# Causal mask of MLA scores: from a matrix product on TensorE into VectorE's row-maximum pass

## The chip, the core and the metric

The kernel runs on one core of one Trainium2 chip. A core has a matrix engine (TensorE, PE in the profile, with its weight loads as PEld), a vector engine (VectorE, DVE), a scalar engine (ScalarE, ACT), a general engine (GpSimd, POOL), and DMA queues that SyncE (SP), ScalarE and GpSimd issue. Each engine works through its own queue in order; semaphores order the engines among each other. The metric is the time of one execution on the device in microseconds (us), as the median of several runs.

## The reference, cut to what matters

The reference computes one layer of a hybrid decoder on 512 tokens of width 1024: a layer norm, a token mixer of gated linear attention (GLA, 4 heads) and multi-head latent attention (MLA, 8 heads) side by side, merged by gates and projected, then a squared-ReLU MLP of hidden width 4096, each with a residual and a layer norm. What the change touches is the causal softmax of MLA:

```python
for blk in range(seq // Q_BLOCK):                  # 4 blocks of 128 queries
    q0, q1 = blk * Q_BLOCK, (blk + 1) * Q_BLOCK
    s = (jnp.einsum('bhqd,bhkd->bhqk', q_nope[:, :, q0:q1], k_nope[:, :, :q1])
         + jnp.einsum('bhqr,bkr->bhqk', q_rope[:, :, q0:q1], k_rope[:, :q1]))
    s = s.astype(jnp.float32) * scale
    mask = (q0 + jnp.arange(Q_BLOCK))[:, None] >= jnp.arange(q1)[None, :]
    p = jax.nn.softmax(jnp.where(mask, s, -jnp.inf), axis=-1).astype(v.dtype)
    outs.append(jnp.einsum('bhqk,bhkv->bhqv', p, v[:, :, :q1]))
```

Block i reads keys 0 to 128(i+1). Only the last 128 of these keys need a mask, the triangle of the diagonal block.

## The kernel before, in words

All large products are made from operands split into a high and a low part: `hi` is the value rounded to TensorE's fp32r format by ScalarE, `lo` the rest by VectorE, and a product is the sum of hi x hi, hi x lo and lo x hi. Products with features on the partitions go through `gemm_fm` (lines 231 to 233), products with tokens on the partitions through `gemm_tm` (lines 264 to 266). Weights are streamed: SyncE's queue loads a block (`wraw`, line 168, three buffers), ScalarE makes `whi` (line 180) and VectorE `wlo` (line 181), two buffers each, while TensorE works on the block before. A block cannot be split before TensorE has freed a buffer.

The stages follow each other: input norm and latents, the GLA projections with the GLA heads between them, the gates, the output projection of GLA (`y_gla`), the MLA heads in four pairs, the output projection of MLA (`y_mla`), the merge, and the MLP. The heads are Python generators: `tick` advances them between the products of the stage's projections, so that TensorE always has projection products to fill in with. That gives each instruction its place in program order; a planner then writes the queue of each engine by priority and by its own estimate of the times, and gives out the buffers. All instructions are unrolled, and the order in which an engine works is fixed before the run.

An MLA head is `mla_head`. For each of the 4 query blocks it makes a score tile of 128 queries by n = 128, 256, 384 or 512 keys in a PSUM bank (pool `px`, four banks that the transposes share): five products at lines 830 to 834, of the two parts without and the two parts with rotation. The sixth product, line 835, adds the mask to the diagonal block: the identity in bf16 (`identb`) times `negb`, a bf16 table of 0 and -1e30. VectorE takes the negated row maximum `mx` from the bank (line 837). ScalarE takes exp(score + mx) from the bank into an SBUF tile `Pm` (line 840) and sums the rows on the way (`sme`). VectorE inverts the sum (line 841) and scales the tile (line 842). TensorE transposes the tiles (line 854), they are split, and the products with the values follow (lines 873 to 875). `Pm` comes from the pool B of 22 buffers of 128 x 512 fp32; blocks 0 and 2 share one.

`identb` is made by ScalarE at the start (line 393) from the constants, `negb` by VectorE in `prep` (line 418) from `neg`, a 128 x 128 fp32 table that comes by DMA in `cb`.

`lmask` (line 400) holds the level masks of GLA as bytes, 7 levels x 2 x 2 x 64 = 1792 bytes per partition. VectorE fills it in two casts at line 912 and reads it in the GLA heads (lines 652 and 685). The GLA heads are finished by `finish(*t_gla)`, line 974, before `y_gla(0)`; the MLA heads begin behind that.

Of the kernel before, what the change touches and what calls it, by code (L numbers as in the profile page):

```python
# [10 lines left out]
F32 = mybir.dt.float32  # L11
F32R = mybir.dt.float32r
BF = mybir.dt.bfloat16
I32 = mybir.dt.int32
U8 = mybir.dt.uint8
AF = mybir.ActivationFunctionType
ALU = mybir.AluOpType
AX = mybir.AxisListType

P = 128  # L20
T = 512
# [25 lines left out]
LEVELS = (1, 2, 4, 8, 16, 32, 64)  # L47
# [5 lines left out]
def tile_hybrid_block(ctx: ExitStack, tc: tile.TileContext, I, out, dbg=None):  # L53
    nc = tc.nc
    dbg = dbg or {}
    consts = ctx.enter_context(tc.tile_pool(name="consts", bufs=1))
# [8 lines left out]
    def nm(s):  # L65
        uid[0] += 1
        return f"{s}_{uid[0]}"
# [4 lines left out]
    def A(shape, dt=F32, n="a"):  # L72
        tag, bufs = ("C", 8) if n in TAG_C else (n, TAG_W[n]) if n in TAG_W else ("A", 24)
        return pa.tile(shape, dt, tag=tag, bufs=bufs, name=nm(n))

    def B(shape, dt=F32, n="b"):
        return pb.tile(shape, dt, tag="B", name=nm(n))

    def S(shape, dt=F32, n="s"):
        return sm.tile(shape, dt, tag=n, name=nm(n))  # L80
# [4 lines left out]
    def PX(shape=(P, T), dt=F32, n="px"):  # L85
        return px.tile(list(shape), dt, tag="px", name=nm(n))
# [4 lines left out]
    act = nc.scalar.activation  # L91
# [4 lines left out]
    mm = nc.tensor.matmul  # L96
# [7 lines left out]
    def split(src, hi, lo, scale=None):  # L104
        if scale is None:
            act(hi, src, AF.Copy)
            return vtt(lo, src, f(hi), op=ALU.subtract)
        else:
            act(hi, src, AF.Copy, scale=scale)
            return stt(lo, src, scale, f(hi), op0=ALU.mult, op1=ALU.subtract)  # L110
# [13 lines left out]
    ident = ca[:, 0:P]  # L124
# [2 lines left out]
    mhalf = consts.tile([P, 8], F32, name="mhalf")  # L127
    nc.vector.memset(mhalf, -0.5)
    identr = consts.tile([P, P], F32R, name="identr")
    identb = consts.tile([P, P], BF, name="identb")  # L130
    negb = consts.tile([P, P], BF, name="negb")


    stream = []
# [65 lines left out]
    def step(g):  # L200
        try:
            next(g)
        except StopIteration:
            active.remove(g)
# [7 lines left out]
    def finish(*gs):  # L212
        while any(g in active for g in gs):
            for g in list(active):
                if g in gs:
                    step(g)
# [173 lines left out]


    act(identr, ident, AF.Copy)
    act(identb, ident, AF.Copy)
    cb = consts.tile([P, PACK_B], F32, name="cb")
    nc.scalar.dma_start(cb, I["c_pack_b"])
    cut = np.cumsum([0, 3, 2, NK, GH, 2 * NK, NK, NK, P, 32]).tolist()
    qag, kvg, glg, bga, bgt, ln1g, ln1b, neg, invf = [cb[:, cut[i]:cut[i + 1]] for i in range(9)]
    posi = consts.tile([P, NT], I32, name="posi")
    nc.scalar.dma_start(posi, I["positions"].rearrange("(t p) -> p t", p=P))
    lmask = consts.tile([P, len(LEVELS), 2, 2, 64], U8, name="lmask")  # L400
    lmi = A([P, 2, len(LEVELS), 64], I32, "lmi")
    nc.scalar.dma_start(lmi[:, 0], I["c_lmask"])
    wa2 = B([80, T], F32, "wa2")
# [7 lines left out]
    def prep():  # L411
        with tc.issue_after(st["pow"].ins):
            nc.gpsimd.memset(lmi[:, 1], 0)
        for li, s in enumerate(LEVELS):
            nc.gpsimd.dma_start(lmi[s:, 1, li], I["c_lmask"][:P - s, li])
        with tc.issue_after(last_in.ins):
            vts(hbg, bgt, 0.5, None, op0=ALU.mult)
            nc.vector.tensor_copy(negb, neg)
        posf = consts.tile([P, NT], F32, name="posf")
        with tc.issue_after(last_in.ins):  # L420
            nc.vector.tensor_copy(posf, posi)
        ang = B([P, NT, 32], F32, "ang")
        for tt in range(NT):
            vts(ang[:, tt, :], invf, posf[:, tt:tt + 1], None, op0=ALU.mult)
        yield
        angs = []
        for sh in (0.0, 0.25):
            kq = B([P, NT, 32], F32, "kq")
            vts(kq, ang, 1.0 / (2.0 * math.pi), sh, op0=ALU.mult, op1=ALU.add)
            vts(kq, kq, MAGIC, None, op0=ALU.add)  # L430
            vts(kq, kq, MAGIC, None, op0=ALU.subtract)
            r = B([P, NT, 32], F32, "rr")
            stt(r, kq, -TWO_PI_1, ang, op0=ALU.mult, op1=ALU.add)
            stt(r, kq, -TWO_PI_2, r, op0=ALU.mult, op1=ALU.add)
            stt(r, kq, -TWO_PI_3, r, op0=ALU.mult, op1=ALU.add)
            vts(r, r, sh * 2.0 * math.pi, PI_F, op0=ALU.add, op1=ALU.min)
            vts(r, r, -PI_F, None, op0=ALU.max)
            angs.append(r)
            yield
        act(sn2[:, :, 32:], angs[0], AF.Sin)  # L440
        act(cs2[:, :, :32], angs[1], AF.Sin)
        nc.vector.tensor_copy(cs2[:, :, 32:], cs2[:, :, :32])
        vts(sn2[:, :, :32], sn2[:, :, 32:], -1.0, None, op0=ALU.mult)
        yield
# [325 lines left out]
    scale = HQ ** -0.5  # L770
# [47 lines left out]
    def mla_head(h, hl, qn, kn, vt):  # L818
        for _ in range((0 if h == MH - 1 else STAG) * hl):
            yield  # L820
        KK, qs = KKs[0], QS[h]
        Ps = []
        P02 = B([P, T], F32, "P02")
        for i in range(NT):
            n = P * (i + 1)
            nn = max(n, 2 * P)
            c = slice(i * P, (i + 1) * P)
            p = PX()
            o = p[:, :nn]
            mm(o, qn[:, 0, c], kn[:, 0, :nn], start=True, stop=False)  # L830
            mm(o, qn[:, 0, c], kn[:, 1, :nn], start=False, stop=False)
            mm(o, qn[:, 1, c], kn[:, 0, :nn], start=False, stop=False)
            mm(o, qs[:, c], KK[:, 0, :nn], start=False, stop=False)
            mm(o, qs[:, c], KK[:, 1, :nn], start=False, stop=False)
            mm(p[:, c], identb, negb, start=False, stop=True)
            mx = S([P, 1], F32, "mx")
            nc.vector.tensor_reduce(mx, p[:, :n], axis=AX.X, op=ALU.max, negate=True)
            Pm = P02[:, :P] if i == 0 else P02[:, P:] if i == 2 else B([P, T], F32, "Pm")
            sme = S([P, 1], F32, "sme")
            act(Pm[:, :n], p[:, :n], AF.Exp, bias=mx, accum_out=sme)  # L840
            nc.vector.reciprocal(sme, sme)
            vts(Pm[:, :n], Pm[:, :n], sme, None, op0=ALU.mult)
            Ps.append(Pm)
            if i != 0:
                yield

        PT = [A([P, 2, T], F32R, "PT0"), A([P, 2, T], F32R, "PT1"), B([P, 2, 256], F32R, "PT2")]
        plan_t = ([(i, 0, i) for i in range(4)], [(i - 1, 1, i) for i in range(1, 4)] + [(3, 3, 3)],
                  [(i - 2, 2, i) for i in range(2, 4)])
        for b, (pl, pt) in enumerate(zip(plan_t, PT)):  # L850
            n = len(pl) * P
            p = PX()
            for cc, j, i in pl:
                nc.tensor.transpose(p[:, cc * P:(cc + 1) * P], Ps[i][:, j * P:(j + 1) * P], ident)  # L854
            split(p[:, :n], pt[:, 0, :], pt[:, 1, :])
            if b != 1:
                yield
        PT0, PT1, PT2 = PT
        while vt[NT - 1] is None:
            yield  # L860
        o = PX()
        for j in range(NT):
            c = slice(hl * P, (hl + 1) * P)
            vh, vl = vt[j][:, 0, c], vt[j][:, 1, c]
            if j == 0:
                ph, pl, od = PT0[:, 0, :], PT0[:, 1, :], o
            elif j == 1:
                ph, pl, od = PT1[:, 0, :384], PT1[:, 1, :384], o[:, 128:]
            elif j == 2:
                ph, pl, od = PT2[:, 0, :], PT2[:, 1, :], o[:, 256:]  # L870
            else:
                ph, pl, od = PT1[:, 0, 384:], PT1[:, 1, 384:], o[:, 384:]
            mm(od, vh, ph, start=j == 0, stop=False)
            mm(od, vh, pl, start=False, stop=False)
            mm(od, vl, ph, start=False, stop=j == NT - 1)
        yield
        om = A([P, 2, T], F32R, "omT")
        st["om"] = split(o, om[:, 0, :], om[:, 1, :])
        omT[h] = om
# [17 lines left out]
    for hf in range(2):  # L897
        if hf == 1:
            finish(t_ln1)
            t_prep = spawn(prep())  # L900
        for i in range(2):
            gemm_tm([PL["lat", i]], hT, half, ev_lat(i), tts=(2 * hf, 2 * hf + 1))
# [46 lines left out]
    def y_gla(mb):  # L949
        def ev_y(a, ps):  # L950
            g = gt[mb * 4 + a]
            stt(g[:, 0, :], g[:, 0, :], 1.0, ps, op0=ALU.add, op1=ALU.mult)
        gemm_fm(PL["yg", mb], ogT, T, ev_y)
# [18 lines left out]
    omT_lazy = Lazy()  # L972

    finish(*t_gla)
    WID[0] = 2
    y_gla(0)
    WID[0] = 4
# [330 lines left out]
```

## Time and profile before

| | before |
|---|---|
| median of 3 runs | 894.29 us (894.25 to 894.30) |
| the profiled execution | 893.91 us |
| its span, first to last instruction | 891.8 us |
| mean clock granted to TensorE | 0.997 |
| TensorE busy | 869.8 us, 98% of the span |
| VectorE busy | 579.0 us, 65% |
| ScalarE busy | 432.2 us, 48% |
| GpSimd busy | 170.7 us, 19% |
| mask products, line 835 | 32, from 357.6 to 461.2 us |

A row of the profile that groups instructions names the line, the engine and the operation, then out<-in by the names of the program's tiles, the shapes, the count, and behind the bar the busy time in us, the mean duration of one in ns, and the idle time of the engine just before them with what ended it. A row of one line's instructions (`L835 PE MATMUL ... x32: 218/230/232`) gives minimum, median and maximum in ns. A row of the timeline gives start and duration in us, the engine, the line, the operation and the tiles; two products of TensorE overlap, so the distance of their starts says more than a duration. A row of the waits reads: engine, tile and line that waited, whom it waited for, us in total, how many times, the longest.

### The profile page before, as it was taken

What the parts mean: (1) busy time and instruction counts of PE and PEld (TensorE: products, weight loads), DVE (VectorE), ACT (ScalarE), POOL (GpSimd) and SP (SyncE); (2) the same over time, 40 slices, a digit from 0 to 9 for tenths busy, and PEclk for the clock granted to TensorE, in tenths of its full rate; (3) what the DMA queues carried; (4) which work ended last, traced back from release to release, by engine and by line L of the source; (5) the groups of instructions that cost most, each with busy time, mean ns of one, the idle gap of its engine ahead of it and who ended that gap; (6) DMA issues with size and microseconds to landing.
All of it is one profiled execution on the core that took longest, in us unless ns stands there. A gap on an engine that the chain in (4) does not pass through costs nothing.

```text
span 891.8 us, 11595 instructions
## 1 busy us (share of the span) xinstructions
PE 869.8 (98%) x4384; PEld 738.2 (83%) x4384; DVE 579.0 (65%) x956; ACT 432.2 (48%) x735; POOL 170.7 (19%) x209
## 2 busy tenths in 40 slices
PE   5999999999999999999999999999999999999995
PEld 4988888888888888888888888988888888888884
DVE  7834875767735235557756797997557646754687
ACT  5546543545434334435644423366357546645661
POOL 0203441433502010000000002104400520242022
PEclk9999999999999999999999999999999999999998
DMA  7513223221213233111307518005950991398065
GB/s 227 150 48 95 72 72 95 72 72 53 79 54 99 69 99 101 54 42 54 100 19 283 190 50 304 1 1 138 305 124 16 262 254 36 67 307 193 1 181 102
DMA packets 63270, 101.13 MB, mean 113 GB/s; under 512 B 7761, under 2 KB 31748, under 8 KB 63216
## 3 DMA queue, kind: packets, MB, share of 16 engines
q1 hardware_dynamic: 48256, 64.04, 23.2%
q0 software_dynamic: 13040, 32.71, 15.3%
q10 hardware_dynamic: 1920, 3.66, 1.2%
q8 instruction: 34, 0.56, 0.3%
q14 instruction: 20, 0.16, 0.1%
HBM read 82.56 MB, written 3.67 MB: 97 GB/s over the span
## 4 chain that ended last, share of the span: by engine, by line
PE 95%; DMA 2%; DVE 1%; issue 0%; ACT 0%; SPq 0%; POOLq 0%; DVEq 0%; POOL 0%; ACTq 0%
PE mm L231 16%; PE mm L233 16%; PE mm L232 16%; PE mm L264 5%; PE mm L266 5%; PE mm L265 5%; PE px L1153 3%; PE px L1154 3%; PE px L1155 3%; PE mm L1154 2%; PE mm L1155 2%; PE mm L1153 2%; DMA wraw<-in_w_in_dram 1%; PE px L692 1%; PE px L854 1%; PE px L266 1%
## 5 line engine op out<-in xcount | busy, mean ns | idle before, releaser
L181 DVE TENSOR_TENSOR wlo<-wraw,whi 128x1024 fp32r<-128x1024 f32 (+1 forms) x104 | 117.5, 1130 | 160.0 <-ACT whi L180 150.3
L231 PE MATMUL mm<-h,whi 128*128 128x512 f32 x416 | 162.8, 393 | 0.0
L232 PE MATMUL mm<-h,whi 128*128 128x512 f32 x416 | 162.2, 390 | 0.0
L180 ACT ACTIVATE whi<-wraw 128x1024 fp32r<-128x1024 f32 (+1 forms) x104 | 100.3, 964 | 127.5 <-PE mm L232 65.0
L233 PE MATMUL mm<-h,wlo 128*128 128x512 f32 x416 | 155.3, 390 | 0.0
L1181 POOL DMA_DIRECT2D res<-ev x54 | 47.8, 975 | 237.1 <-ACT ev L1179 186.9
L233 PEld LDWEIGHTS mm<-h,wlo 128*128 128x128 f32 x416 | 78.1, 188 | 16.1
L231 PEld LDWEIGHTS mm<-h,whi 128*128 128x128 f32 x416 | 78.2, 188 | 15.8
L232 PEld LDWEIGHTS mm<-h,whi 128*128 128x128 f32 x416 | 78.2, 188 | 15.5
L265 PE MATMUL mm<-wlo,h 128*128 128x512 f32 x128 | 50.6, 395 | 0.0
L266 PE MATMUL mm<-whi,h 128*128 128x512 f32 x128 | 50.2, 394 | 0.0
L264 PE MATMUL mm<-whi,h 128*128 128x512 f32 x128 | 49.9, 400 | 0.0
L1235 ACT ACTIVATE relu<-mm 128x512 f32<-128x512 f32 x32 | 18.8, 596 | 57.2 <-PE mm L233 57.2
L352 POOL TENSOR_TENSOR mv<-mv,mhalf 128x1 f32<-128x1 f32 x4 | 4.6, 1153 | 211.5 <-DVE mv L351 211.5
L618 POOL TENSOR_TENSOR rp<-rp 128x256 f32<-128x256 f32 x32 | 29.9, 935 | 63.5 <-ACT E L636 52.8
L643 DVE TENSOR_TENSOR M<-E,qk 128x256 f32<-128x256 f32 x48 | 28.9, 628 | 12.4 <-ACT E L636 12.1
L636 ACT ACTIVATE E<-rp 128x512 f32<-128x512 f32 x32 | 20.4, 638 | 26.2 <-POOL rp L619 26.1
L180 ACT ACTIVATE xh<-wraw 128x1024 fp32r<-128x1024 f32 (+1 forms) x20 | 18.9, 963 | 26.3 <-PE mm L266 16.3
L181 DVE TENSOR_TENSOR wlo<-wq,whi 128x1024 fp32r<-128x1024 f32 x15 | 18.4, 1224 | 19.7 <-ACT whi L180 19.7
L266 PEld LDWEIGHTS mm<-whi,h 128*128 128x128 f32 x128 | 24.1, 188 | 4.8
L265 PEld LDWEIGHTS mm<-wlo,h 128*128 128x128 f32 x128 | 24.1, 188 | 4.4
L264 PEld LDWEIGHTS mm<-whi,h 128*128 128x128 f32 x128 | 23.9, 188 | 4.2
(381 smaller groups left out, 2241.9 us busy)
## 6 DMA issues: line engine op xcount, KB each, us to landing
wraw<-in_w_in_dram SPq DMA_DIRECT2D x40, 512.0 KB, 3.6
wraw<-in_w_ff_dram SPq DMA_DIRECT2D x32, 512.0 KB, 7.7
wq<-in_w_ff_dram POOLq DMA_DIRECT2D x32, 512.0 KB, 9.2
res<-ev POOLq DMA_DIRECT2D x54, 256.0 KB, 8.5
wraw<-in_w_o_gla_dram SPq DMA_DIRECT2D x8, 512.0 KB, 3.7
wraw<-in_w_o_mla_dram SPq DMA_DIRECT2D x8, 512.0 KB, 3.4
wraw<-in_w_out_dram SPq DMA_DIRECT2D x8, 512.0 KB, 4.3
wraw<-in_w_in_dram SPq DMA_DIRECT2D x8, 360.0 KB, 3.7
```

Source lines behind the costliest of these rows:

```text
L180: st["ins"] = act(hi[:, :nk, :n], raw[:, :nk, :n], AF.Copy)
L181: vtt(lo[:, :nk, :n], raw[:, :nk, :n], f(hi[:, :nk, :n]), op=ALU.subtract)
L231: mm(o, hi[:, c], xh, start=first, stop=False)
L232: mm(o, hi[:, c], xl, start=False, stop=False)
L233: mm(o, lo[:, c], xh, start=False, stop=last)
L264: mm(o, xh, hi[:, :n], start=opens, stop=False, skip_group_check=share)
L265: mm(o, xh, lo[:, :n], start=False, stop=False, skip_group_check=share)
L266: mm(o, xl, hi[:, :n], start=False, stop=last, skip_group_check=share)
L1153: mm(o, xh[:, c], hi[:, pp, cols], start=opens, stop=False, skip_group_check=True)
L1154: mm(o, xh[:, c], lo[:, pp, cols], start=False, stop=False, skip_group_check=True)
L1155: mm(o, xl[:, c], hi[:, pp, cols], start=False, stop=hf == 1 and pp == 1, skip_group_check=True)
L1181: nc.gpsimd.dma_start(res[tt + t][:, j * T:(j + 1) * T], e, accum_op=ALU.add)
```

## The change

The mask is no longer a product. A table `cmask` of 128 x 512 fp32 holds 0 in its first 384 columns and `neg` in the last 128, so that its last n columns are the mask of a block with n keys. One VectorE instruction, `tensor_tensor_reduce`, replaces the reduction: it reads the scores from PSUM and the last n columns of the table from SBUF, writes -(score + mask) into `Pm`, and folds the minimum of what it writes, which is the negated row maximum, into `mx`, from the start value 3e38. The exponential then reads `Pm` in SBUF with scale -1 and writes it in place. The bank is read by nobody else, so it is free after VectorE's instruction. The fifth score product closes the sum in the bank.

`identb`, `negb` and the two instructions that made them go. The table and the level masks share one tile: `lmask` is a view of the first 1792 of `cmask`'s 2048 bytes per partition. After `finish(*t_gla)` GpSimd sets the first 384 columns to zero and copies `neg` into the last 128.

```diff
-    identb = consts.tile([P, P], BF, name="identb")
-    negb = consts.tile([P, P], BF, name="negb")
+    cmask = consts.tile([P, T], F32, name="cmask")
...
     act(identr, ident, AF.Copy)
-    act(identb, ident, AF.Copy)
...
-    lmask = consts.tile([P, len(LEVELS), 2, 2, 64], U8, name="lmask")
+    nl = len(LEVELS)
+    lmask = cmask.bitcast(U8)[:, :nl * 256].rearrange("p (l o u i) -> p l o u i", l=nl, o=2, u=2)
...
             vts(hbg, bgt, 0.5, None, op0=ALU.mult)
-            nc.vector.tensor_copy(negb, neg)
...
             mm(o, qs[:, c], KK[:, 0, :nn], start=False, stop=False)
-            mm(o, qs[:, c], KK[:, 1, :nn], start=False, stop=False)
-            mm(p[:, c], identb, negb, start=False, stop=True)
+            mm(o, qs[:, c], KK[:, 1, :nn], start=False, stop=True)
             mx = S([P, 1], F32, "mx")
-            nc.vector.tensor_reduce(mx, p[:, :n], axis=AX.X, op=ALU.max, negate=True)
             Pm = P02[:, :P] if i == 0 else P02[:, P:] if i == 2 else B([P, T], F32, "Pm")
+            nc.vector.tensor_tensor_reduce(Pm[:, :n], p[:, :n], cmask[:, T - n:], -1.0, 3.0e38,
+                                           op0=ALU.add, op1=ALU.min, accum_out=mx)
             sme = S([P, 1], F32, "sme")
-            act(Pm[:, :n], p[:, :n], AF.Exp, bias=mx, accum_out=sme)
+            act(Pm[:, :n], Pm[:, :n], AF.Exp, scale=-1.0, bias=mx, accum_out=sme)
...
     finish(*t_gla)
+    nc.gpsimd.memset(cmask[:, :T - P], 0.0)
+    nc.gpsimd.tensor_copy(cmask[:, T - P:], neg)
     WID[0] = 2
     y_gla(0)
```

## The prediction

> **What bounds the kernel now.** I read the page's busy times and its chain first.
>
> ```profile
> span 891.8 us, 11595 instructions
> PE 869.8 (98%) x4384; PEld 738.2 (83%) x4384; DVE 579.0 (65%) x956; ACT 432.2 (48%) x735; POOL 170.7 (19%) x209
> PE 95%; DMA 2%; DVE 1%; issue 0%; ACT 0%; SPq 0%; POOLq 0%; DVEq 0%; POOL 0%; ACTq 0%
> ```
>
> TensorE is busy for 98% of the span and carries 95% of the chain that ends last. A microsecond of other engines counts only where TensorE then waits. Next comes the stage that the change touches, by stretches (columns: length, then busy time and count of PE, PEld, DVE, ACT and POOL, the clock, the DMA share, GB/s).
>
> ```profile
> 355.00:400.00 45.00, 45.00 (x242) 37.95 (x242) 26.01 (x53) 18.10 (x41) 0.00 (x0) 1.00 0.18 53
> 400.00:430.00 30.00, 30.00 (x188) 26.09 (x188) 21.31 (x52) 16.54 (x43) 0.00 (x0) 1.00 0.26 76
> 430.00:446.00 16.00, 16.00 (x102) 13.84 (x102) 13.47 (x34) 10.26 (x25) 0.00 (x0) 1.00 0.24 75
> 446.00:465.00 19.00, 19.00 (x114) 16.07 (x113) 12.03 (x35) 8.80 (x27) 0.00 (x0) 1.00 0.06 21
> ```
>
> The reader is to see that TensorE has no idle time at all here, at full clock, while VectorE is free for 19.0, 8.7, 2.5 and 7.0 us of the four stretches. So TensorE's work sets the time of the stage, and the third stretch is where VectorE has least to spare. The mask products and the reductions that follow them:
>
> ```profile
> L835 PE MATMUL px<-negb,identb x32: 218/230/232, 357.6 to 461.2; 128*128 128x128 bf16 x32
> DVE mx L837 <- PE px L835: 9.3, 11, 2.3
> ACT Pm L840 <- DVE mx L837: 10.5, 12, 3.1
> ```
>
> There are 32 of them, one for each of 8 heads and 4 query blocks. VectorE waits for TensorE and ScalarE for VectorE here, never the other way round.
>
> **The change, part by part.**
>
> *The 32 mask products go.* The 230 ns of a row above overlap with the neighbours, so what one costs is read from the starts on TensorE.
>
> ```profile
> 357.52 0.28 PE L834 MATMUL px<-KK,QS 128*128 128x256 f32 x1
> 357.64 0.23 PE L835 MATMUL px<-negb,identb 128*128 128x128 bf16 x1
> 357.68 0.36 PE L831 MATMUL px<-qn,qn 128*128 128x256 f32 x1
> 357.88 0.28 PE L832 MATMUL px<-qn,qn 128*128 128x256 f32 x1
> 358.00 0.28 PE L833 MATMUL px<-KK,QS 128*128 128x256 f32 x1
> ...
> 461.21 0.23 PE L835 MATMUL px<-negb,identb 128*128 128x128 bf16 x1
> 461.24 0.47 PE L231 MATMUL mm<-omT,whi 128*128 128x512 f32 x1
> 461.56 0.39 PE L232 MATMUL mm<-omT,whi 128*128 128x512 f32 x1
> 461.78 0.39 PE L233 MATMUL mm<-omT,wlo 128*128 128x512 f32 x1
> ```
>
> Two 256-column products stand 0.12 us apart (357.88 to 358.00). From the start of the mask product to the start of the second one after it are 0.24 us, and 0.12 of these belong to the 256-column product in between: the mask costs 0.12. At the last of the 32 it is 0.35 less the 0.22 to 0.23 that a 512-column product takes: 0.12 to 0.13. Over the 30 places that can be read this way the mean is 0.123 us. The product itself takes about 0.04 of that (357.64 to 357.68); the rest is the next product, 0.36 long in place of 0.28. Without the mask, L834 is followed by its successor as L833 is by L834, at the successor's own rate. So 32 x 0.123 = 3.9 us go. Bounds: a 128-column product on the plain rate would be half of 0.12, 1.9 us in all; the whole recorded duration, 32 x 0.23 = 7.4 us, is the most. The start-to-start reading lies between and is the only one of what TensorE really lost, so I take 3.9.
>
> *The row maximum becomes a pass that adds the table, negates and writes the tile.* The nearest rows are the reduction itself, the two-operand passes from PSUM and SBUF into SBUF, and, for a second instruction that would fetch the minimum, one-column instructions.
>
> ```profile
> L837 DVE TENSOR_REDUCE mx<-px 128x1 f32<-128x512 f32 x8 | 5.5, 688 | 2.5 <-PE px L835 2.4
> L107 DVE TENSOR_TENSOR PT<-px,PT 128x512 fp32r<-128x512 f32 x12 | 7.9, 685 | 4.1 <-ACT PT L106 4.1
> L181 DVE TENSOR_TENSOR wlo<-wraw,whi 128x512 fp32r<-128x512 f32 x9 | 6.2, 688 | 7.0 <-ACT whi L180 5.1 <-PE mm L232 1.9
> L841 DVE RECIPROCAL sme<-sme 128x1 f32<-128x1 f32 x32 | 5.1, 160 | 4.9 <-ACT Pm L840 3.2 <-ACT P L840 1.3
> L840 ACT ACTIVATION_READ_ACCUMULATOR Pm<-px,mx 128x1 f32 x16 | 3.1, 195 | 0.0
> L837 DVE TENSOR_REDUCE mx<-px 128x1 f32<-128x128 f32 (+3 forms) x32 | 15.6, 487 | 9.4 <-PE px L835 9.3
> ...
> 430.00:446.00 16.00, 3.24 (x7) 1.00 0.24 75
> ```
>
> Reading a second operand costs a pass nothing (685 against 688 ns at 512 columns). I take the same pass as before, mean 487 ns, plus a fetch of 0.16 us, the one-column row of VectorE; the ends are no fetch at all (0) and, since no such accumulating pass is in this trace, twice the pass and a fetch of 0.195 (0.68 us more a tile). With the value taken VectorE has 32 x 0.16 = 5.1 us more, spread as the reductions are. The last row above counts the reductions of the third stretch, 7; the same view has 8, 10 and 8 in the others (one is counted on both sides of a bound). So VectorE gets 1.3, 1.6, 1.1 and 1.3 us more, against 19.0, 8.7, 2.5 and 7.0 us free. It costs TensorE nothing. If that cover went, the first to be late would be a head's transposes, where the margin can be read.
>
> ```profile
> 462.50 0.48 DVE L842 TENSOR_SCALAR Pm<-Pm,sme 128x512 f32<-128x512 f32 x1
> ...
> 463.25 0.49 DVE L842 TENSOR_SCALAR Pm<-Pm,sme 128x512 f32<-128x512 f32 x1
> ...
> 464.08 0.27 PE L854 MATMUL px<-ca,P 128*128 128x128 f32 x1
> ```
>
> The first of heads 6 and 7 has its last tile at 462.98 and TensorE first asks at 464.08, 1.1 us later. The four tiles of heads 6 and 7 just before would add 4 x 0.16 = 0.64 us. Behind the new pass on VectorE's queue stand those scalings and the low halves of weight blocks (L181), for which TensorE waits next.
>
> *The exponential reads the tile from SBUF instead of PSUM.* Copies show the difference by source:
>
> ```profile
> L180 ACT ACTIVATE whi<-wraw 128x512 fp32r<-128x512 f32 x9 | 5.7, 631 | 7.0 <-PE mm L232 4.1 <-issue 2.9
> L106 ACT ACTIVATE PT<-px 128x512 fp32r<-128x512 f32 x12 | 6.7, 593 | 5.6 <-PE px L854 5.6
> ```
>
> That is 0.04 us more for each of 32, 1.2 us on an engine that is idle 13 of the 30 us and 6 of the 16 us of its fullest stretches: nothing for TensorE. In return the score bank is given back after VectorE's pass instead of after the exponential. TensorE waits for no bank now, so I count no gain. The SBUF tile is taken one pass earlier, before the maximum; a wait for a free one would stall VectorE's queue, but nothing in the trace shows such a wait, bounds 0 to one scaling of 0.5 us a head.
>
> *The table moves into the level masks' memory, filled by GpSimd after the gated attention.*
>
> ```profile
> L652 DVE COPY_PREDICATED SD<-lmask,px x24: 422/444/740, 108.7 to 246.8; 128x256 f32<-128x256 uint8 x24
> 329.86 0.78 POOL L450 TENSOR_TENSOR rt<-rt,rt 128x256 f32<-128x256 f32 x1 [1.16 <-DVE rt L449]
> L611 POOL MEMSET rp<- 128x512 f32 x4 | 2.1, 527 | 0.0
> ```
>
> The masks are last read at 247.2 us, and the first score tile comes at 357.9. GpSimd's last work before that ends at 330.6, and in the stretches above it does nothing. The fill (at most 0.53, the row of a larger memset) and the copy (at most 0.8, the row of a wider addition) fit the 27 us between. Even in front of the rope additions they would delay these by 1.3 us, and each of those waits for VectorE anyway. It issues no DMA and moves past none. Cost: 0.
>
> *The two bf16 copies at the start go:* one instruction of ScalarE, one of VectorE.
>
> ```profile
> L393 ACT ACTIVATE identb<-ca x1: 293/293/293, 4.2 to 4.2; 128x128 bf16<-128x128 f32 x1
> ...
> 8.00 1.24 ACT L356 ACTIVATE x<-x,nmr,mvin 128x1024 f32<-128x1024 f32 x1 [3.51 <-DVE nmr L355]
> 16.84 0.22 DVE L418 CAST negb<-cb 128x128 bf16<-128x128 f32 x1
> 17.52 0.69 DVE L349 BATCH_NORM_STATS2 bst<-x 128x6 f32<-128x512 f32 x1 [0.38 <-DMA x<-in_x_dram]
> ```
>
> ScalarE's copy ends before a 3.5 us wait, VectorE's before a wait for a load of x: both gains, 0.3 and 0.2 us, go into these waits. 0.
>
> **Sum.** The profiled execution took 893.91 us around its span of 891.8; less 3.9 gives 890.0. The median of the runs is 894.29, 0.38 above it, so I predict 890.3. TensorE stays full from the stage to the last products, so the 3.9 us travel to the end.
>
> **The rivals.**
>
> *The pass is twice as long.* Then the third stretch gets 7 x (0.487 + 0.16) = 4.5 us more, 13.47 becomes 18.0 in 16 us, and 2.0 us come back: 892.3. The others still fit (21.3 + 6.5 in 30, 12.0 + 5.2 in 19). For it: the trace has no accumulating pass. Against it: no pass from PSUM with a second operand is longer than its columns make it. The Trainium skill, Vector Engine (DVE) Microarchitecture Reference, section Points that are easy to get wrong, says that a two-tensor instruction with an accumulator runs at half rate when both sources are non-bf16 in SBUF. Read to the letter it spares this pass, whose scores lie in PSUM; no run here shows it yet. Chance 0.06.
>
> *The gain is partly given back by a new order.* The planner writes every queue again. If TensorE now comes to each head's transposes 0.3 us before the scaled tile (two fetches of 0.16), 8 heads return 2.6 us: 892.9. Against it stands the margin of 1.1 us above. Chance 0.12.
>
> *Slower: weight blocks come late.* A block's split takes ScalarE and VectorE a whole pass each:
>
> ```profile
> L181 DVE TENSOR_TENSOR wlo<-wraw,whi 128x1024 fp32r<-128x1024 f32 x6 | 7.3, 1223 | 2.1 <-ACT whi L180 2.0
> L180 ACT ACTIVATE whi<-wraw 128x1024 fp32r<-128x1024 f32 x5 | 5.3, 1068 | 6.0 <-issue 3.6 <-PE mm L266 1.8 <-ACT Pm L840 0.7
> ```
>
> If the new order puts softmax work ahead of a split, so that TensorE arrives before it begins, a block costs 1.07 + 1.22 = 2.3 us. Two such blocks (4.6) eat the gain; with three, 890.3 + 6.9 = 897.2. For it: TensorE's order is fixed and ScalarE already waits for TensorE to free the buffers. Against it: TensorE shows no such wait in the whole stage, and VectorE has room. Chance 0.12.
>
> *The products were hidden anyway,* and the next product takes their 0.12 us, waiting for its own weights: 894.3. Against it: L833 to L834, with the same kind of weights, keep 0.12. Chance 0.06.
>
> **How the numbers follow.** The forecast has 0.64, with a range of its own from 889.3 (a few tenths from sooner banks) to 891.6. About 0.2%, 1.8 us, is what a measurement tells from no change, so faster means below 892.5. Faster: nearly all of 0.64, half of the doubled pass, a third of the new order: 0.70. Same: the rest of these and the hidden products: 0.18. Slower: 0.12. The range 889.3 to 894.4 leaves out the late blocks and a little below.
>
> **What would show it.** Right: no L835; L834 followed at 0.12 to 0.23 us; TensorE's busy time down by 4 to 7 us with its idle time in the stage still zero; a VectorE pass of about 0.49 us mean and something short behind it; everything after the stage 3.9 us earlier. Wrong: a wait of TensorE for a scaled tile or a low half between 355 and 480, a pass near 1 us, or a wait of GpSimd's fill that holds up the first tile.

## The result and the profile after

The changed kernel takes 890.03 us (median of 6 runs, 889.20 to 890.38); the kernel before, run beside it, takes 894.25 us. The ratio is 0.9952, with a 95% interval of 0.9942 to 0.9962: 4.2 us faster. The profiled execution took 889.94 us, against 893.91 before.

The page of the kernel after, its span, its busy times and its chain:

```profile
span 888.0 us, 11561 instructions
PE 866.7 (98%) x4352; PEld 738.3 (83%) x4352; DVE 578.2 (65%) x987; ACT 432.7 (49%) x734; POOL 173.8 (20%) x211
PE 95%; DVE 2%; DMA 2%; issue 1%; ACT 0%; POOLq 0%; SPq 0%; POOL 0%; DVEq 0%; ACTq 0%
```

Of TensorE's products exactly 32 are gone (4384 to 4352), and it still carries 95% of the chain. The span is 3.8 us shorter. The stage in which this happens can be marked off by two landmarks: the first score product (356.3 us before, 356.4 after) and the last transposes of the residual rows `res` behind the output products (568.1 before, 564.4 after). So the stage shrank from 211.8 to 208.1 us, by 3.7; what lies ahead of it (356.4 against 356.3) and behind it (323.6 against 323.7) is nearly unchanged.

The same four stretches as before, in the view of busy times by stretch of the kernel after (columns: length, then busy time and count of PE, PEld, DVE, ACT and POOL, the clock, the DMA share, GB/s):

```profile
355.00:400.00 45.00, 45.00 (x242) 38.64 (x241) 26.09 (x62) 18.42 (x42) 0.00 (x0) 1.00 0.18 54
400.00:430.00 30.00, 30.00 (x185) 26.97 (x184) 21.54 (x65) 18.22 (x48) 0.00 (x0) 1.00 0.31 90
430.00:446.00 16.00, 16.00 (x98) 14.32 (x97) 12.74 (x37) 8.80 (x21) 0.00 (x0) 1.00 0.21 71
446.00:465.00 19.00, 18.97 (x111) 16.47 (x111) 13.36 (x44) 11.26 (x29) 0.00 (x0) 1.00 0.00 1
```

TensorE is still full at full clock, with 0.03 us of idle time in 110. VectorE's sum over the four went from 72.8 to 73.7 us only. The planner has written the queues anew, though: apart from the removed products, TensorE's order differs in some 75 places, and the first product of the MLA projection with `omT` comes at 441.9 us in place of 444.8.

The joints between two score tiles, in the timeline of TensorE after the change (start, duration):

```profile
357.48 0.28 PE L831 MATMUL px<-KK,QS 128*128 128x256 f32 x1
357.49 0.19 PEld L832 LDWEIGHTS px<-KK,QS 128*128 128x128 f32 x1
357.60 0.28 PE L832 MATMUL px<-KK,QS 128*128 128x256 f32 x1
357.61 0.19 PEld L829 LDWEIGHTS px<-qn,qn 128*128 128x128 f32 x1
357.72 0.28 PE L829 MATMUL px<-qn,qn 128*128 128x256 f32 x1
357.84 0.28 PE L830 MATMUL px<-qn,qn 128*128 128x256 f32 x1
```

The fifth product (L832) is followed by the next tile's first (L829) after 0.12 us, and that by its successor after 0.12. The 0.24 us from the mask product to the second one behind it have become 0.12.

The new pass and the exponential, by line and form, in the groups of the stretch from 355 to 466 us (behind the bar: busy us, mean ns of one); the first row is the exponential of the kernel before, the others are of the kernel after:

```profile
L840 ACT ACTIVATE Pm<-px,mx 128x512 f32<-128x512 f32 x8 | 5.5, 688 | 7.6 <-DVE mx L837 7.6
L838 ACT ACTIVATE Pm<-Pm,mx 128x512 f32<-128x512 f32 x8 | 5.8, 725 | 11.6 <-DVE mx L835 11.6
L835 DVE CUSTOM_DVE_ANT_0 Pm<-px,cmask 128x512 f32<-128x512 f32 x8 | 5.5, 686 | 4.6 <-PE px L832 4.5
L835 DVE CUSTOM_DVE_ANT_0 P<-px,cmask 128x384 f32<-128x384 f32 x8 | 4.4, 550 | 0.5 <-PE px L832 0.5
```

And the instruction that fetches the minimum, in the view of line 835:

```profile
L835 DVE DVE_READ_ACCUMULATOR2_ANT mx<- x32: 79/83/85, 358.1 to 461.3; 128x1 f32 x32
```

The pass that adds, negates, writes and folds takes 686 ns at 512 columns, where the bare reduction took 688. It needs a fetch of 83 ns behind it. The exponential is 37 ns longer from SBUF than from PSUM (725 against 688).

GpSimd's fill, in its timeline after the change:

```profile
246.36 0.42 POOL L973 MEMSET cmask<- 128x384 f32 x1 [0.96 <-DVE SD L650]
247.36 1.28 POOL L974 COPY cmask<-cb 128x128 f32<-128x128 f32 x1 [0.57 <-DVE SD L650]
248.60 0.73 POOL L710 TENSOR_TENSOR sd<-SD,sd 128x256 fp32r<-128x256 f32 x1
```

The fill waits for the last reads of the level masks, as the program asks, and the planner has put it ahead of the last GLA head's additions (L710), which ended at 249.0 us before and end at 249.3 now.

### The profile page after: what moved, and what is told of

Its sections match the earlier page's. It is cut to its first block, busy times and chain, and to the rows that moved or that the text cites. A ratio compares the mean times of both kernels' runs of the same rounds, so it can differ in the third digit from the quotient of the medians.

```text
span 888.0 us, 11561 instructions
## 1 busy us (share of the span) xinstructions
PE 866.7 (98%) x4352; PEld 738.3 (83%) x4352; DVE 578.2 (65%) x987; ACT 432.7 (49%) x734; POOL 173.8 (20%) x211
## 4 chain that ended last, share of the span: by engine, by line
PE 95%; DVE 2%; DMA 2%; issue 1%; ACT 0%; POOLq 0%; SPq 0%; POOL 0%; DVEq 0%; ACTq 0%
PE mm L230 16%; PE mm L232 16%; PE mm L231 16%; PE mm L263 5%; PE mm L265 5%; PE mm L264 5%; PE px L1153 3%; PE px L1155 3%; PE px L1154 3%; PE mm L1153 2%; PE mm L1155 2%; PE mm L1154 2%; PE px L690 1%; DMA x<-in_x_dram 1%; PE px L852 1%; PE px L265 1%
```

## The experiments

The experiments were timed in five rounds against the kernel before, whose medians in them lie between 893.93 and 894.06 us. "Stage" is the distance between the two landmarks in the profiled execution, "waits" what TensorE waited for another engine inside the stage, in us. Left out is a wait of 0.3 us for `h` of the layer norm near the stage's end, which every one of these kernels has, the one before too.

| kernel | median us | ratio to before (95%) | stage us | waits |
|---|---|---|---|---|
| before | 894.25 | 1 | 211.8 | none |
| after | 890.03 | 0.9952 (0.9942 to 0.9962) | 208.1 | none |
| e1: after + a 128-column product | 894.25 | 1.0006 (0.9998 to 1.0015) | 212.4 | 0.4 |
| e3: after + a 64-column product | 893.75 | 0.9998 (0.9990 to 1.0007) | 211.7 | none |
| e4: after + a 256-column product | 895.01 | 1.0014 (1.0002 to 1.0026) | 212.0 | none |
| e2: before, no mask at all | 890.08 | 0.9961 (0.9948 to 0.9973) | 207.8 | none |
| e8: after, block 0 narrow | 889.97 | 0.9958 (0.9945 to 0.9970) | 207.7 | none |
| e5: the pass twice | 894.33 | 1.0006 (0.9997 to 1.0015) | 211.5 | 2.1 and 0.5 |
| e7: diagonal added on its own | 894.58 | 1.0009 (1.0000 to 1.0018) | 211.8 | 1.8 and 0.7 |
| e10: e7, scaling on ScalarE | 893.78 | 0.9999 (0.9990 to 1.0008) | 211.8 | 1.8 and 0.7 |
| e11: add, then reduce from SBUF | 893.82 | 1.0002 (0.9993 to 1.0011) | 213.1 | 1.5, 0.8, 0.4 |
| e9: unrelated additions | 891.99 | 0.9979 (0.9969 to 0.9988) | 208.1 | none |
| e12: an addition off the chain | 891.31 | 0.9971 (0.9962 to 0.9980) | 208.6 | 0.5 |
| e13: e7, later weight splits | 894.63 | 1.0007 (0.9998 to 1.0016) | 211.8 | 1.8 and 0.7 |

### Is the whole gain TensorE's time?

e1 puts a product without effect back into the changed kernel: the identity times a table of zeros.

```diff
-            mm(o, qs[:, c], KK[:, 1, :nn], start=False, stop=True)
+            mm(o, qs[:, c], KK[:, 1, :nn], start=False, stop=False)
+            mm(p[:, c], identb, zb, start=False, stop=True)
```

> The changed kernel with the 32 products put back on TensorE: the same shape and weights (identity in bf16, 128 columns), but a table of zeros, so the VectorE pass still makes the mask. Everything else of the change stays. My theory (the whole gain is TensorE time, 0.123 us a product, 3.9 us in all): the time goes back to 893.9, within 0.5 of the kernel before. Rival A (a part of the gain comes from the score bank that is free sooner, or from the pass itself): it stays between 890.5 and 893. Rival B (the products were hidden and the gain is a matter of the planner's new order): it stays at 890.

Measured: 894.25 us, the time of the kernel before. The mask in VectorE's pass, the score bank that comes free sooner and the exponential from SBUF are all still there, and nothing of the gain is left. The products were not hidden.

e2 goes the other way: the kernel before without its mask product, everything else as it was. It leaves out the mask.

```diff
-            mm(o, qs[:, c], KK[:, 1, :nn], start=False, stop=False)
-            mm(p[:, c], identb, negb, start=False, stop=True)
+            mm(o, qs[:, c], KK[:, 1, :nn], start=False, stop=True)
```

> The kernel before without the mask product, and with no mask in its place (the causal mask is left out, so the softmax runs over the whole of the diagonal block); reduction, exponential from PSUM and the bank held until then as before. My theory: 893.91 to 894.3 less 3.9, so 890.3, the same as the changed kernel within 0.5: the new pass costs nothing and the sooner bank gains nothing. Rival A (the pass costs some time on the way to TensorE): this is faster than the changed kernel, 888 to 889.5. Rival B (the sooner bank is part of the gain): this is slower than the changed kernel, 891 to 893.

Measured: 890.08 us, within 0.05 of the changed kernel; the stage is 0.3 us shorter (207.8). So the new pass and the sooner bank together change next to nothing: a kernel that does not mask at all, reduces and exponentiates from PSUM, is no faster by its median. That each of the two alone is nothing is not shown.

### What sets the price of such a product?

e3 and e4 repeat e1 with 64 and 256 moving columns in place of 128.

```diff
-            mm(p[:, c], identb, zb, start=False, stop=True)
+            mm(p[:, i * P:i * P + 64], identb, zb, start=False, stop=True)
```

> The changed kernel with a bf16 product of the identity put back into each tile, as in the run that put back all 128 columns (894.25), but with 64 columns of zeros. The prediction read 0.04 us for the product and the rest for its successor, which can load its own weights only once this product has begun. By that theory half the columns save at most half of 0.04, and the cost stays near 0.10 to 0.12 us: 893.3 to 894.2. Rival (the cost goes with the columns): half of 3.9 comes back, 892.0.

> The same with 256 columns of zeros. Theory (the successor's weight load sets the cost until the columns take longer than it): 256 columns stand 0.12 us apart elsewhere, so the cost stays at 0.12 to 0.13 us and the time at 894.0 to 894.5. Rival (cost goes with the columns): twice 3.9, so 898.

TensorE's timeline at the first of them, with 64 columns:

```profile
357.51 0.28 PE L836 MATMUL px<-KK,QS 128*128 128x256 f32 x1
357.63 0.10 PEld L837 LDWEIGHTS <-identb 128*128 128x128 bf16 x1
357.63 0.20 PE L837 MATMUL px<-zb,identb 128*128 128x64 bf16 x1
357.64 0.20 PEld L833 LDWEIGHTS px<-qn,qn 128*128 128x128 f32 x1
357.68 0.36 PE L833 MATMUL px<-qn,qn 128*128 128x256 f32 x1
357.88 0.28 PE L834 MATMUL px<-qn,qn 128*128 128x256 f32 x1
```

and with 256:

```profile
357.85 0.28 PE L837 MATMUL px<-zb,identb 128*128 128x256 bf16 x1
357.89 0.36 PE L833 MATMUL px<-qn,qn 128*128 128x256 f32 x1
358.09 0.28 PE L834 MATMUL px<-qn,qn 128*128 128x256 f32 x1
```

In both the product itself takes 0.04 us and its successor 0.20 in place of 0.12. Read as in the prediction, the cost is 0.12 us with 64 columns and with 256, as with the 128 columns of the kernel before. From 64 to 256 it does not depend on the columns. The rows show what it comes with: without the product the successor's weight load starts 0.11 to 0.12 us ahead of the successor (L829 at 357.61 and 357.72 in the changed kernel), with it only 0.04 ahead (L833 at 357.64 and 357.68). This speaks for the additional weight load as the cause; no run varied the weights alone. A rival is the change of type, from fp32r to bf16 and back. The changed kernel's own trace speaks against bf16 as the reason: a transpose of 128 fp32 columns that stands alone between wider products has the same pattern.

```profile
368.97 0.27 PE L852 MATMUL px<-ca,Pm 128*128 128x128 f32 x1
369.00 0.36 PE L831 MATMUL px<-KK,QS 128*128 128x256 f32 x1
369.20 0.28 PE L832 MATMUL px<-KK,QS 128*128 128x256 f32 x1
```

Its successor comes after 0.03 us and holds on for 0.20 in place of 0.12. At 13 such places between 365 and 463 us the transpose costs 0.11 to 0.12 us. The median of e4, 895.01 us, lies above what was expected (894.0 to 894.5) and 1.3 us above that of e3 where the stages differ by 0.3; that remainder is not explained.

e8 asks whether the columns of the score products still have something to give. Block 0 needs 128 keys and computes 256.

```diff
-            nn = max(n, 2 * P)
+            nn = n
```

> The changed kernel with the five score products of query block 0 at 128 columns instead of 256 (half of their columns are never read): 40 products. If a product never costs less than the 0.12 us that its successor's weight load takes (as 64, 128 and 256 columns in the mask product did, 0.124, 0.124 and 0.123), nothing is gained: 890.0 within 0.4, at most 0.6 less by the 0.108 at which 128-column transposes follow each other. Rival (cost by the columns): 40 x 0.06 = 2.4 less, 887.6. Rival (fp32r products narrower than 256 columns run slower): 891 or more.

Measured: 889.97 us, 0.06 below the changed kernel, which its interval does not tell apart. The 128-column products start mostly 0.11 us apart, where 256 columns take 0.12: halving the columns of these products saves next to nothing.

### What if the pass were longer?

The prediction's first rival was a pass of twice the length. e5 makes it so by issuing it twice.

```diff
             nc.vector.tensor_tensor_reduce(Pm[:, :n], p[:, :n], cmask[:, T - n:], -1.0, 3.0e38,
                                            op0=ALU.add, op1=ALU.min, accum_out=mx)
+            nc.vector.tensor_tensor_reduce(Pm[:, :n], p[:, :n], cmask[:, T - n:], -1.0, 3.0e38,
+                                           op0=ALU.add, op1=ALU.min, accum_out=mx)
```

> The changed kernel with the new VectorE instruction issued twice for every tile, with the same result: 32 x (0.485 + 0.083) = 18.2 us more on VectorE in the MLA stage, all of it ahead of the exponential. By the prediction's second case the stretch with least room overflows: with the measured 12.7 us busy of 16 and 7 tiles, 12.7 + 4.0 = 16.7, so some 0.7 to 2.0 us come back, 891 to 892. Rival (the planner spreads the work, and VectorE's free time is one pool over the stage: 110 less 73.7 = 36 us): no change, 890.0 within 0.4. Second rival (each head's chain is on the way to TensorE, 8 heads x 4 tiles x 0.57): more than 895.

Measured: 894.33 us; all of the gain is gone, against 0.7 to 2.0 us that were expected. What TensorE waited for in the stage:

```profile
PE px L873 <- DVE PT L107: 2.1, 1, 2.1
PE px L828 <- DVE PT L107: 0.5, 1, 0.5
```

Both waits end with the VectorE instruction that takes the low half of the transposed probabilities `PT` (line 107). Neither product reads that half: line 828 multiplies queries and keys, line 873 values and the high half. The buffers that the planner gave out show what they wait for: in the programs of e5, e7, e10 and e13 both products write the PSUM bank that the transposes filled, and line 107 is the last to read it. The long wait lies in the stretch that the prediction named (430 to 446 us), but VectorE is not full there:

```profile
430.00:446.00 16.00, 13.88 (x89) 12.53 (x88) 14.67 (x47) 9.66 (x23) 0.00 (x0) 1.00 0.22 68
```

VectorE works 14.67 of 16 us. The waits are 2.6 of the 3.4 us by which the stage is longer than after. Another 0.9 us between the two profiled executions lie ahead of the stage (first score product at 357.2 us), where none of the doubled passes has run.

e7 replaces the product in the simplest way: an addition of its own on the diagonal's 128 columns, in the bank, with reduction and exponential as in the kernel before.

```diff
-            mm(o, qs[:, c], KK[:, 1, :nn], start=False, stop=False)
-            mm(p[:, c], identb, negb, start=False, stop=True)
+            mm(o, qs[:, c], KK[:, 1, :nn], start=False, stop=True)
+            vtt(p[:, c], p[:, c], neg, op=ALU.add)
             mx = S([P, 1], F32, "mx")
```

> The kernel before without the mask product; the mask is added by a VectorE instruction of its own, in PSUM, to the 128 columns of the diagonal block, and the reduction and the exponential from PSUM stay as they were. VectorE gets 32 x 0.29 = 9.2 us more instead of the 2.7 of the fetch. My theory (any form that takes the products off TensorE gains them whole while VectorE has room): 890.3 within 0.5. Rival (the fused pass matters, since a separate instruction adds a wait between it and the reduction and TensorE's next tiles come late): 891.5 to 893.

Measured: 894.58 us. This was a miss: 890.3 had been expected, and the rival's 893 at most. The addition takes 0.29 us a tile:

```profile
L835 DVE TENSOR_TENSOR px<-px,cb 128x128 f32<-128x128 f32 x32 | 9.3, 292 | 5.5 <-PE px L834 5.4
```

and brings the same two waits, in the view of the waits of e7:

```profile
PE px L873 <- DVE PT L107: 1.8, 1, 1.8
PE px L830 <- DVE PT L107: 0.7, 1, 0.7
```

e7 differs from e2 in this one instruction, and the stage is 3.9 us longer (211.8 against 207.8). By the starts on TensorE some 3.3 of them lie at the two waits, where the products just behind also stand further apart than usual. So fusing the mask into the pass is what made the change worth while: 32 products off TensorE, paid with 0.29 us a tile ahead of the exponential, give nothing.

### Load, bank or place?

Three explanations were open for e5 and e7: VectorE has too much to do; the score bank is held longer; or the tile arrives later at the transposes, and what follows on the queues makes the delay larger.

*Load.* e10 is e7 with the scaling moved from VectorE to ScalarE.

```diff
-            vts(Pm[:, :n], Pm[:, :n], sme, None, op0=ALU.mult)
+            act(Pm[:, :n], Pm[:, :n], AF.Copy, scale=sme)
```

> The kernel with the mask addition of its own (894.58), and with the scaling by the inverted row sum moved from VectorE to ScalarE: 32 passes of 0.28 to 0.49 us, 12.3 us, off VectorE, some 16 us more on ScalarE. Theory (VectorE's load between 425 and 446 us is what took the gain): it comes back, 890.3 within 0.7, with no wait of TensorE for the low half of PT. Rival (the longer chain): it stays at 894, as the chain is as long as before or longer.

```profile
430.00:446.00 16.00, 14.25 (x90) 12.71 (x90) 11.95 (x30) 12.37 (x31) 0.00 (x0) 1.00 0.21 67
```

VectorE now works 11.95 of 16 us there, less than in the changed kernel (12.74), and the waits are the same 1.8 and 0.7 us, the stage the same 211.8. So VectorE's load does not make the waits here. ScalarE works more, though, 12.37 of 16 us, so e10 alone leaves open that its load has taken over. (Its median is 0.8 us below that of e7, but the profiled executions, 893.28 and 893.32, do not differ.)

e9 wanted the opposite, the load without the place: the changed kernel with an addition that reads only the table and that nobody reads.

```diff
+            vtt(scr, neg, neg, op=ALU.add)
```

> The changed kernel plus one VectorE addition of 128 columns of the mask table for each tile, into a scratch tile that nobody reads: about 0.28 us x 32 = 9 us more on VectorE, as much as the mask addition of its own brought, but outside the chain from scores to exponential. Theory (VectorE's free time between 425 and 446 us is used up, so any work there delays the low halves of the transposed tiles): the gain goes again, 893 to 894.5, with TensorE waiting for the low half of PT between 425 and 446. Rival (it was the longer chain, scores to addition to reduction): no loss, 890.0 within 0.5.

It failed as an experiment. Since the addition waits for nothing, the planner put all 32 at the very start (5.7 to 45.4 us), among the work of the input norm and the latents. The first score product comes at 358.6 us, 2.3 later than after; the stage is 208.1, and 891.99 us says nothing on the question.

e12 ties the same addition to its place: it reads the scaled tile, so it stands behind the scaling, and nobody waits for it.

```diff
             vts(Pm[:, :n], Pm[:, :n], sme, None, op0=ALU.mult)
+            vtt(scr, Pm[:, n - P:n], neg, op=ALU.add)
```

> The changed kernel plus one VectorE addition of 128 columns for each tile into a scratch tile that nobody reads, reading the scaled tile, so that it can run only in the MLA stage (the side work of the run before reads only the table, and all 32 of it ran before 45.4 us, so it said nothing on this stage). 9 us more on VectorE there, no bank held longer, the chain to the exponential as it is. Theory A (bank held longer took the gain) and the theory of the chain: 890.0 within 0.7. Theory C (VectorE's load takes it): 892.5 to 894.5, with TensorE waiting behind the low half of PT.

The view of waits and the busy times by stretch of e12:

```profile
PE px L829 <- DVE PT L107: 0.5, 1, 0.5
```

```profile
430.00:446.00 16.00, 16.00 (x100) 14.37 (x99) 14.37 (x45) 9.81 (x24) 0.00 (x0) 1.00 0.26 84
```

VectorE works 14.37 of 16 us, more than in e7 (13.67), and TensorE is full. The stage is 208.6. An addition of the same size, 32 times, costs the stage 0.5 us behind the scaling (e12 against after), all of it one wait, and 3.9 ahead of the exponential (e7 against e2). The median, 891.31 us, fits neither forecast (890.7 at most, or 892.5 at least); it holds another 0.5 us ahead of the stage, where the first score product comes at 356.9 us.

*Bank.* e11 is the changed kernel with its pass cut in two: an addition from PSUM into the SBUF tile, which frees the bank as early as the changed kernel does, then a reduction from SBUF.

```diff
-            nc.vector.tensor_tensor_reduce(Pm[:, :n], p[:, :n], cmask[:, T - n:], -1.0, 3.0e38,
-                                           op0=ALU.add, op1=ALU.min, accum_out=mx)
+            vtt(Pm[:, :n], p[:, :n], cmask[:, T - n:], op=ALU.add)
+            nc.vector.tensor_reduce(mx, Pm[:, :n], axis=AX.X, op=ALU.max, negate=True)
```

> The changed kernel with the fused instruction cut in two: an addition from PSUM and the table into the SBUF tile, then the row maximum from the SBUF tile; the exponential reads the tile. VectorE does as much and the chain is as long as with the pass issued twice (894.33, TensorE waiting 0.5 and 2.1 us near 427 and 442 us), but the score bank is free after the first of the two. Theory A (TensorE waited there for a bank, and a bank held longer is what took the gain): no such wait, 890.3 within 0.7. Theory B (VectorE's queue or the length of the chain to the exponential took it): 893.5 to 894.5, with the same two waits.

```profile
PE px L872 <- DVE PT L107: 1.5, 1, 1.5
PE px L828 <- DVE PT L107: 0.8, 1, 0.8
PE px L871 <- ACT PT L106: 0.4, 1, 0.4
```

The waits are there with the score bank freed early: it is not the score bank. Nor is it the transposes' bank alone: the values' products of e11 write another one, and they wait for `PT` itself, 0.4 us for the high half (line 871) and 1.5 for the low one (line 872). In both cases the last of the waiting ends when line 107 has run. The remaining explanation is that the tiles come later to the transposes and the halves of `PT`.

*Place.* What turns 0.29 us a tile into a wait of 1.8 us shows in the two timelines of ScalarE and VectorE around 440 us. The changed kernel:

```profile
437.14 1.09 ACT L106 ACTIVATE PT<-px 128x512 fp32r<-128x512 f32 x2 [0.40 <-PE px L852]
437.78 1.29 DVE L107 TENSOR_TENSOR PT<-px,PT 128x512 fp32r<-128x512 f32 x2 [0.45 <-ACT PT L106]
439.34 1.09 ACT L179 ACTIVATE whi<-wraw 128x1024 fp32r<-128x1024 f32 x1
439.44 0.39 PE L871 MATMUL px<-PT,mv 128*128 128x512 f32 x1
440.99 1.22 DVE L180 TENSOR_TENSOR wlo<-wraw,whi 128x1024 fp32r<-128x1024 f32 x1
```

and e7:

```profile
439.16 0.60 PE L854 MATMUL px<-ca,Pm 128*128 128x128 f32 x4
439.30 1.06 ACT L180 ACTIVATE whi<-wraw 128x1024 fp32r<-128x1024 f32 x1 [0.22 <-ACT Pm L840]
440.26 1.06 ACT L106 ACTIVATE PT<-px 128x512 fp32r<-128x512 f32 x2
440.39 1.22 DVE L181 TENSOR_TENSOR wlo<-wraw,whi 128x1024 fp32r<-128x1024 f32 x1 [0.73 <-ACT whi L180]
441.74 1.28 DVE L107 TENSOR_TENSOR PT<-px,PT 128x512 fp32r<-128x512 f32 x2
442.47 0.50 PE L873 MATMUL px<-PT,mv 128*128 128x512 f32 x1 [1.83 <-DVE PT L107]
```

After the change the halves of `PT` go first on both engines, and the weight block behind them. In e7 the transposes come two microseconds later, the weight block's split has been put ahead of the halves of `PT`, and these stand behind 1.06 us on ScalarE and 1.22 on VectorE. The same order, weights ahead of `PT` at this point, is in the traces of e5, e10, e11 and e13, which all have the wait; `PT` ahead of the weights is in those of all the other kernels, which do not.

e13 was to move that split in e7 behind the halves, by making the block due only when TensorE's code reaches it.

```diff
+    for key in (("qn", 2), ("qn", 3), ("ym", 0)):
+        stream[PL[key]["idx"][0]]["ahead"] = 0
```

> The kernel with the separate diagonal addition (no mask product, `neg` added to the diagonal 128 columns in the bank by a pass of its own), with one thing changed: the first weight block behind each of the guards of pairs 1 to 3 (qn of pairs 2 and 3, and the first block of the MLA projection) is split into its high and low half only when TensorE's code reaches it, behind the heads' own halves, and no longer one block ahead. Theory (place in the queue): the stall of the diagonal addition comes from those splits (1.06 us on ScalarE, 1.22 on VectorE) standing ahead of the heads' halves of PT. Then the waits of the values' first product near 442 us (1.8) and of the score product near 427 us (0.7) for the low half of PT go, and the time falls from 894.6 to 890.3 to 892.0; some tenths of a wait for the weights themselves may take their place. Rival (the chain from scores to exponential is simply too long): the same two waits stand, and the time stays at 894.0 to 894.8. A third way, that the split now comes too late: the PT waits go, but TensorE waits up to 2.3 us for whi or wlo at each of the three places, and the time is 894 or more.

Measured: 894.63 us, the same two waits. But the edit did not do what it was for: the planner gave ScalarE and VectorE the same order as in e7, from 300 to 560 us, split first:

```profile
439.18 1.06 ACT L180 ACTIVATE whi<-wraw 128x1024 fp32r<-128x1024 f32 x1 [0.22 <-ACT Pm L842]
440.15 1.06 ACT L106 ACTIVATE PT<-px 128x512 fp32r<-128x512 f32 x2
441.62 1.28 DVE L107 TENSOR_TENSOR PT<-px,PT 128x512 fp32r<-128x512 f32 x2
```

So it decides nothing. What is shown: an addition of 0.29 us ahead of the exponential takes the gain (e7 against e2), and neither VectorE's load (e10, e12) nor the score bank (e11) is the reason. Not shown is whether the longer chain does it by itself or by the order that the planner then writes, since every run with the longer chain has the weights ahead of `PT` too. That the split's place on the two queues makes most of the wait is read from the traces only. An estimate of its share from e7's rows: the transposes end at 439.76, the first high half takes about 0.6 us, so VectorE could begin the low halves near 440.4 in place of 441.74; some 1.3 of the 1.8 us would go. No run has shown it.

## Why the prediction was right, step by step

*The products, 3.9 us.* Right. The stage lost 3.7 us, the profiled execution 3.97, the medians 4.2; e1 takes all of it away again. The reading by starts was the right one of the three: neither the plain rate (1.9) nor the recorded duration (7.4) comes near. e3 and e4 add what the prediction only guessed from the successor's 0.36 us: the price is not that of 128 columns but the same from 64 to 256, as an additional weight load's would be; that it is the load is argued, not shown.

*The pass.* The main part was right (686 against the 688 ns taken from the reduction). The term that was mis-sized is the fetch: 0.083 us and not 0.16, so 2.7 us more for VectorE in all and not 5.1. It changed nothing, since TensorE stayed full. The reason given, that VectorE has free time for it, was not the right one: it would let the 0.29 us a tile of e7 pass as well, and these cost the whole gain. That the cost came out at 0 as forecast was in part luck, as the fetch is short; no run shows what 0.16 us would have done. The half-rate rule that the prediction cited from the Trainium skill, Vector Engine (DVE) Microarchitecture Reference, section Points that are easy to get wrong, speaks of two sources in SBUF, and this pass has one in PSUM; the trace agrees that it is spared, with 686 ns. No run here had an accumulating pass with both sources in SBUF.

*The exponential from SBUF, 0.04 us; no gain from the sooner bank.* Right: 0.037, and e2, without the sooner bank (and without the fetch), is as fast.

*The fill.* The cost of 0 was right, its working not in every point. The memset (0.42) was within its bound of 0.53, the copy (1.28) was beyond the 0.8 taken from a wider addition (one of the shorter of its line, the others take up to 1.64), and the planner put both ahead of the last GLA head's addition, whose end moved by 0.3 us. What hides it is what the prediction said of the rope additions: GpSimd's next work, at line 747, waits for VectorE, for 19.9 us, and begins at 269.20 us, against 269.15 before.

*The copies at the start, 0.* The first score product moved by 0.1 us.

*What would show it.* No L835 product, the 0.12 us behind the fifth product, no new idle time in the stage, and the earlier end came as written. TensorE's busy time was said to fall by 4 to 7 us and fell by 3.1, outside that range. In the stage it fell by 3.8; ahead of it TensorE waited 0.6 us less in all and was busy 0.7 us more, with the first score product at nearly the same time.

*The rivals.* None came about, but two of them were priced wrongly, and e5 and e7 show how. For the doubled pass the prediction counted VectorE's work in the third stretch against its free time: 18.0 in 16 us, so 2.0 back. The run gave 4.3 back, 3.4 of it in the stage, with VectorE at 14.67 of 16. The place was right and the mechanism was not: the sum of the work does not decide, and what is left is when the tiles reach the transposes. With 0.29 us more a tile, 1.2 us for the four tiles of a head, the kernel is already over the edge; the margin of 1.1 us that the prediction read at heads 6 and 7 was a better guide than the free time, though the wait comes at the heads before. The rival of the late weight blocks saw the right pieces, 1.07 and 1.22 us of a split on the two queues, in the wrong order: in e7 it is not softmax work that delays a split, but a split that stands ahead of softmax work.

The products hidden anyway are refuted by e1. The new order did come, in some 75 places, and gave nothing back.

## What to carry to other kernels

Where TensorE is full, read the price of a small product from the starts of its neighbours and not from its columns or its duration; here a small product between wider ones cost 0.12 us, from 64 to 256 columns. Ask what the replacement of work taken off TensorE adds to the chain that leads back to TensorE: here, as part of a pass that ran anyway, the mask was free, and as a pass of 0.29 us it ate the whole gain. Free time of an engine in a stretch does not say that a chain through it has room: look for the margin at the first instruction that waits for the chain's end, and for what the engine's queue may put ahead of it.

## What the runs showed that was not expected

- The price of an inserted product, 0.12 us with 64, 128 and 256 columns alike.
- The accumulator's fetch on VectorE, 0.083 us, is half of the 0.16 us of a one-column instruction there.
- GpSimd's copy of 128 x 128 fp32 took 1.28 us, while its addition of 128 x 256 beside it (L710) took 0.73. It is one copy, and the same addition took 1.26 us in the kernel before.
- After its waits TensorE did not always come back at full clock: in e11 the granted clock was 0.91 in the stretch from 430 to 446 us, with two 512-column products 0.43 us apart where 0.23 is usual. This is a part of e11's stage of 213.1 us, 1.6 more than e5's.
- The beginning of the MLA stage moves: the first score product stands between 356.0 and 358.6 us in these runs. It need not be the edit: e1 and e3 differ in the zeros' columns alone and have it at 358.1 and 356.3 us, and near 33 us TensorE waited 2.3 us for `h` in the one and 0.7 in the other. A median alone, without the stage's own length, would have misread e9 by 2 us.
